# Neighbourhood heads of a two-layer encoder: borders transposed together, high and low parts stacked in one product, meta columns in one product

## The chip, the core and the metric

One program on one core of a Trainium2 chip. The metric is device time in microseconds of one execution, as the median of several; smaller is better. Beside it stands one profiled execution, whose span runs from the first to the last instruction of the program. The engines are PE (TensorE; PEld is its weight load), ACT (ScalarE), DVE (VectorE), POOL (GpSimd) and SP (SyncE, which issues nearly all DMAs).

## What is computed

Two layers over 512 grid tokens (8 rows by 64 columns) and 16 meta tokens, D = 1024. Each layer has a global attention branch (A), a neighbourhood attention branch (B), gates, and two output projections. The change lies in branch B, here cut to what matters:

```python
def neighbourhood_attention(q, k, v, rpb):          # 8 heads of 64
    # meta queries see the 16 meta keys only
    s_mm = einsum('bqhd,bmhd->bhqm', qm, km) * scale
    o_meta = einsum('bhqm,bmhd->bqhd', softmax(s_mm), vm)
    # a grid query sees a clamped window of 8 rows x 16 columns, with a bias, and the 16 meta keys
    s_win = einsum('bchd,bicjhd->bhcij', q_row, k_win) * scale + bias
    s_meta = einsum('bchd,bmhd->bhcm', q_row, km) * scale
    p = softmax(concatenate([s_win, s_meta], -1))
    o = einsum(p_win, v_win) + einsum(p_meta, vm)
```

All products are made from float32 values split into a high part (fp32r) and a low part (the remainder), so that `x*y` is high*high + high*low + low*high.

## The kernel before

**Main stream.** PE runs the projections (`product`, tiles `pp` and `y`, lines 391 to 393): for each chunk of 128 output columns, eight 128-row pieces times three products, into a bank of 256 and one of 272 tokens in layer 0, or one of 512 in layer 1. The weights come by DMA from SP (`raw`, L301), ACT makes the high part (`whi`, L306), POOL the low part (`wlo`, L307). At the end `pf` (L1306 to L1308) makes the last output product.

**Side work.** Two objects of class `Side` drop the attention work between these products. At each `tick` (twice per chunk) parts that are due are emitted. A neighbourhood head starts every fourth tick, and `NA_AT["stages"]` says at which tick after its start each stage is emitted: prepare 0, scores 2, transposes1 4, transposes2 5, transposes3 5, sums 7. Inside one engine the order is the scheduler's, moved at some places by the table `BEHIND`, which puts one named instruction behind another.

**A neighbourhood head** (`windowed_head`, 8 in each layer, 16 in all). The tokens are ordered column by column, so a window is a band. The scores of four blocks of 128 queries against 208, 272, 272 and 208 keys land in PSUM (`Sb`). DVE adds the bias and takes the maximum (L1062), ACT the exponential (L1064), in place in the 128x960 tile `bias`. Then PE transposes the probabilities by products with an identity (`transposed`, L196):

- `ta`: four 128x128 pieces of the inner keys; ACT and DVE split them into `tah` and `tal`.
- `tb`: two more inner pieces, and two of 80 columns from the borders (the first and the last 64 keys, each with a copy of the 16 meta keys); split into `tbh` and `tbl`.
- `tc`: one piece of 64 columns, in which the meta columns of the two inner query blocks lie; `split_meta` (L864 on ACT, L870 on DVE) puts it into the tile `na` with a mask `inner`.
- `tm` (layer 0 alone): the meta queries' own 16x16 probabilities, made from the two products `sm` (L627, L628), go to the tile `mm`.

The stage `sums` (L1124) then adds eleven products into one bank `avb` of 512 queries; the stationary operand is a slice of the values `VB2` (slices 0 to 2 inner, 3 and 4 borders, 5 the meta values). In layer 0 one product more, `avbm` (L1135), makes the meta queries' output. `window_edges` (L811) makes slices 3 to 5 of `VB2` once per pair of heads, from three transpositions `vtc` of 80 columns.

**Buffers around the change.** `na`, `mm`, `pm` are single buffers, zeroed once. The transposed pieces land in the PSUM pool `ps_t` with two banks; `S` and `Sb` share one double bank.

Of the kernel before, what the change touches and what calls it, by code (L numbers as in the profile page):

```python
# [38 lines left out]
NA_AT = ({"stages": (0, 2, 4, 5, 5, 7), "values": (3, 4), "divide": (3, 4, 7)},  # L39
         {"stages": (0, 2, 4, 5, 5, 7), "values": (3, 4), "divide": (3, 4, 7)})  # L40
# [18 lines left out]
BLK = ((0, 0, 208), (480, 64, 272), (208, 208, 272), (752, 336, 208))  # L59
# [3 lines left out]
BLK_META = 448  # L63
# [95 lines left out]
def trunk_kernel(ctx: ExitStack, tc: tile.TileContext, xT, w, gn, gf, bias, rope, out):  # L159
# [72 lines left out]
    for kind, (cols, n, dt) in {"ga": (256, 1, F32R), "na": (256, 1, F32R), "mm": (NMETA, 1, F32R), "pm": (32, 1, F32), "inv": (32, 1, F32)}.items():  # L232
# [9 lines left out]
    inner = cpool.tile([P, 1], F32, name="inner")  # L242
    nc.gpsimd.memset(inner, 1.0)
    nc.gpsimd.affine_select(inner, inner, pattern=[[0, 1]], compare_op=ALU.is_ge, fill=0.0, base=-NMETA, channel_multiplier=1)
    nc.gpsimd.affine_select(inner, inner, pattern=[[0, 1]], compare_op=ALU.is_ge, fill=0.0, base=3 * NMETA - 1, channel_multiplier=-1)
# [1142 lines left out]
```

## Time and profile before

| what | value |
|---|---|
| median of 3 runs | 819.23 us (818.29 to 820.59) |
| the profiled execution, its own time | 818.64 us |
| its span | 816.7 us |
| granted TensorE clock, mean | 0.999 |
| DVE, ACT, POOL busy | 505.2, 473.5, 418.0 us (62%, 58%, 51%) |
| PE products, weight loads | 5658 each |
| DMA moved | 134.99 MB, mean 165 GB/s |

How to read it: a product's record lasts longer than its turn, since the next one starts while it still drains. So the cost of a product on PE is the distance from its start to the start of the next, which the timeline view gives, and not the duration in its row. In timeline rows the columns are start and duration in us, engine, line, operation, tile written and tiles read, shape, and count. Rows with a bar are groups: busy time and mean of one, then idle time of the engine before them.

### The profile page before, as it was taken

What the parts mean: (1) busy time and instruction counts of PE and PEld (TensorE: products, weight loads), DVE (VectorE), ACT (ScalarE), POOL (GpSimd) and SP (SyncE); (2) the same over time, 40 slices, a digit from 0 to 9 for tenths busy, and PEclk for the clock granted to TensorE, in tenths of its full rate; (3) what the DMA queues carried; (4) which work ended last, traced back from release to release, by engine and by line L of the source; (5) the groups of instructions that cost most, each with busy time, mean ns of one, the idle gap of its engine ahead of it and who ended that gap; (6) DMA issues with size and microseconds to landing.
All of it is one profiled execution on the core that took longest, in us unless ns stands there. A gap on an engine that the chain in (4) does not pass through costs nothing.

```text
span 816.7 us, 16071 instructions
## 1 busy us (share of the span) xinstructions
PE 808.8 (99%) x5658; PEld 755.1 (92%) x5658; DVE 505.2 (62%) x1154; ACT 473.5 (58%) x1137; POOL 418.0 (51%) x362
## 2 busy tenths in 40 slices
PE   9999999999999999999999999999999999999997
PEld 9999999999999999999988989998988888888786
DVE  7566767796785662365547666676867655324733
ACT  8645777677865654443445557666758755544322
POOL 1654454454554544655754645554625555556651
PEclk9999999999999999999999999999999999999999
DMA  8347474667645563435555575766775555652602
GB/s 299 108 133 216 145 212 131 183 212 204 184 146 183 159 210 119 142 105 173 153 122 137 141 231 154 213 162 179 194 227 159 171 181 152 198 174 90 206 1 104
DMA packets 113248, 134.99 MB, mean 165 GB/s; under 512 B 31888, under 2 KB 66192, under 8 KB 113168
## 3 DMA queue, kind: packets, MB, share of 16 engines
q1 hardware_dynamic: 112448, 132.90, 54.9%
q8 instruction: 45, 0.74, 0.4%
q10 hardware_dynamic: 720, 1.06, 0.4%
q14 instruction: 35, 0.29, 0.1%
HBM read 98.50 MB, written 21.84 MB: 147 GB/s over the span
## 4 chain that ended last, share of the span: by engine, by line
PE 94%; DMA 2%; ACT 1%; DVE 1%; issue 1%; SPq 1%; POOLq 0%; POOL 0%; DVEq 0%; ACTq 0%
PE pp L393 20%; PE pp L391 20%; PE pp L392 20%; PE av L977 4%; PE y L393 4%; PE y L391 4%; PE y L392 4%; PE avb L1124 2%; PE S L627 2%; PE S L628 2%; PE pf L1306 2%; PE pf L1308 2%; PE pf L1307 2%; PE pp L516 2%; DMA raw<-in_w_dram 1%; PE Sb L628 1%
## 5 line engine op out<-in xcount | busy, mean ns | idle before, releaser
L307 POOL TENSOR_TENSOR wlo<-raw,whi 128x512 fp32r<-128x512 f32 x210 | 284.4, 1364 | 287.1 <-ACT whi L306 223.3
L391 PE MATMUL pp<-hh,whi 128*128 128x256 f32 (+2 forms) x1040 | 325.2, 313 | 0.0
L393 PE MATMUL pp<-hh,wlo 128*128 128x256 f32 (+2 forms) x1040 | 324.1, 312 | 0.0
L392 PE MATMUL pp<-hl,whi 128*128 128x256 f32 (+2 forms) x1040 | 323.4, 311 | 0.0
L393 PEld LDWEIGHTS pp<-hh,wlo 128*128 128x128 f32 x1040 | 195.7, 188 | 10.3
L392 PEld LDWEIGHTS pp<-hl,whi 128*128 128x128 f32 x1040 | 195.7, 188 | 9.3
L391 PEld LDWEIGHTS pp<-hh,whi 128*128 128x128 f32 x1040 | 195.9, 188 | 8.7
L306 ACT CAST whi<-raw 128x512 fp32r<-128x512 f32 x210 | 128.0, 619 | 106.3 <-PE pp L392 36.2
L970 POOL TENSOR_TENSOR ga<-pm,ga 32x128 fp32r<-32x128 f32 x64 | 39.4, 615 | 64.1 <-ACT ga L968 39.9
L939 DVE STREAM_TRANSPOSE P<-P 128x512 f32<-128x512 f32 x64 | 46.5, 727 | 29.8 <-ACT P L913 29.4
L1203 DVE TENSOR_TENSOR mg<-pp,rbc 128x256 f32<-128x256 f32 (+2 forms) x48 | 24.8, 516 | 54.0 <-PE pp L393 53.7
L909 DVE CUSTOM_DVE_ANT_0 P<-S,r 128x528 f32<-128x528 f32 x64 | 44.8, 701 | 15.5 <-PE S L628 14.7
L260 DVE TENSOR_TENSOR ptl<-P,pth 128x512 fp32r<-128x512 f32 x64 | 48.9, 780 | 4.7 <-ACT pth L259 4.2
L913 ACT ACTIVATE P<-P,st 128x528 f32<-128x528 f32 x64 | 47.2, 737 | 1.7
L1064 ACT ACTIVATE bias<-bias,stb 128x208 f32<-128x208 f32 (+1 forms) x64 | 31.0, 485 | 18.2 <-DVE stb L1062 18.2
L1204 ACT ACTIVATE mg<-mg 128x256 f32<-128x256 f32 (+2 forms) x48 | 23.6, 492 | 28.0 <-DVE mg L1203 27.9
L259 ACT CAST pth<-P 128x512 fp32r<-128x512 f32 x64 | 39.3, 614 | 0.9 <-DMA P<-turn 0.8
L392 PE MATMUL pp<-mx,whi 128*128 128x272 f32 (+1 forms) x128 | 36.4, 285 | 0.0
L391 PE MATMUL pp<-mx,whi 128*128 128x272 f32 (+1 forms) x128 | 36.4, 285 | 0.0
L393 PE MATMUL pp<-mx,wlo 128*128 128x272 f32 (+1 forms) x128 | 36.4, 285 | 0.0
L912 ACT ACTIVATE st<-st 128x1 f32<-128x1 f32 x64 | 12.9, 202 | 40.4 <-DVE st L909 40.1
L977 PE MATMUL av<-pth,VA 128*128 128x256 f32 x128 | 34.0, 289 | 0.0
(534 smaller groups left out, 1717.9 us busy)
## 6 DMA issues: line engine op xcount, KB each, us to landing
raw<-in_w_dram SPq DMA_DIRECT2D x210, 256.0 KB
turn<-P SPq DMA_DIRECT2D x32, 528.0 KB
P<-turn SPq DMA_DIRECT2D x128, 128.0 KB
bias<-in_bias_dram SPq DMA_DIRECT2D x16, 480.0 KB
KB<-KB SPq DMA_DIRECT2D x24, 272.0 KB
rawl<-in_w_dram SPq DMA_DIRECT2D x16, 256.0 KB
x<-in_xT_dram SPq DMA_DIRECT2D x8, 264.0 KB
xr<-in_xT_dram SPq DMA_DIRECT2D x8, 264.0 KB
```

Of the source, the lines that this page charges most:

```text
L259: split_at["hi"] = nc.scalar.copy(hi, src)
L260: split_at["any"] = nc.vector.tensor_sub(lo, src, hi.bitcast(F32))
L306: cast = nc.scalar.copy(hi, raw)
L307: sub = nc.gpsimd.tensor_sub(lo, raw, hi.bitcast(F32))
L391: nc.tensor.matmul(ps, wh, rh[:, a:b], start=i == 0, stop=False)
L392: nc.tensor.matmul(ps, wh, rl[:, a:b], start=False, stop=False)
L393: nc.tensor.matmul(ps, wl, rh[:, a:b], start=False, stop=i == n - 1)
L909: newest["max"] = nc.vector.tensor_tensor_reduce(p[:n], joined(S)[:n], scale[:n].to_broadcast([n, NTOK]), 1.0, -3e38, ALU.mult, ALU.max, s ...
L913: nc.scalar.activation(p[:n], p[:n], AF.Exp, bias=st[:n, 1:2], scale=1.0, accum_out=st[:n, 2:3] if total is None else total)
L939: nc.vector.transpose(c["both"][:n, a:b], c["both"][:n, a:b])
L970: nc.gpsimd.tensor_sub(tm[64 + 32 * t:96 + 32 * t, n * t:n * (t + 1)], m, tm[:32, :n].bitcast(F32))
L977: nc.tensor.matmul(c["av"], rows2(c["t"][i][0]), c["t"][i][1], start=i == 0, stop=i == 8)
```

## The change

Key order in a head is turned by half, so that the two borders lie next to each other in the tile `bias` (`BLK`, `ENDS` = 416) and 16-wide pads with the meta keys stay where the first and the inner blocks want them.

- **Borders.** One 128x128 transposition takes both borders (64 columns each) in place of two of 80 columns. Its result is split into the new tile `ne` of two halves: one for each border, with the high part on 64 partitions and the low part on the other 64. `window_edges` makes the slices 3 and 4 of `VB2` with the border's values twice, once on each 64 partitions. So the high and the low part of a border are summed in one product of 128x128, two per head in place of four of 80x128.
- **Metas.** POOL copies the four blocks' meta columns into the new tile `nm` (128x128, L1052 of the new kernel); one transposition of it, the fourth of `tb`, replaces `tc`, and `split_meta` writes four blocks of 16 rows into `na`, now 512 wide. One product of 128x512 in place of one of 128x256 adds all metas. `transposes3` is gone; the mask `inner` too.
- **Meta queries (layer 0).** Their probabilities are written into free columns of `nm`, so `tm` and the tile `pm` are gone; `mm` is filled from the same bank with a mask `upper`. The two products `sm` of 16x16 become one of 16x32 against the high and low keys side by side; ACT copies one half and DVE adds them.
- **Values.** `vtc` is two transpositions (128 and 64 columns) in place of three; ACT copies the halves across partitions.
- **Order.** The table `BEHIND` is written anew.

```diff
-BLK = ((0, 0, 208), (480, 64, 272), (208, 208, 272), (752, 336, 208))
+BLK = ((480, 0, 208), (0, 64, 272), (688, 208, 272), (272, 336, 208))
-BLK_META = 448
+ENDS, META_OF = 416, (1, 3, 0, 2)
...
-            for i, a in enumerate((0, EDGE, HD - NMETA)):
-                nc.tensor.transpose(ps[:EDGE, P * i:P * (i + 1)], v[:, a:a + EDGE], ident)
-            split(out[:EDGE, 3:, :, 0], out[:EDGE, 3:, :, 1], ps[:EDGE, :3 * P].rearrange("p (t h d) -> p t h d", t=3, h=2))
-            nc.scalar.copy(out[HD:, 5], out[:HD, 5].bitcast(F32))
+            nc.tensor.transpose(ps[:, :P], v[:, NKEY - P:], ident)
+            nc.tensor.transpose(ps[:HD, P:2 * P], v[:, :HD], ident)
+            src = ps[:, :2 * P].rearrange("p (t h d) -> p t h d", t=2, h=2)
+            split(out[:HD, 4:, :, 0], out[:HD, 4:, :, 1], src[:HD])
+            split(out[HD:, 3, :, 0], out[HD:, 3, :, 1], src[HD:, 0])
+            nc.scalar.copy(out[HD:, 4:], out[:HD, 4:].bitcast(F32))
+            nc.scalar.copy(out[:HD, 3], out[HD:, 3].bitcast(F32))
...
+                parts = [(slice(32 * i, 32 * i + NMETA), slice(P * b, P * b + P)) for i, b in enumerate(META_OF)]
+                for r, q in parts:
+                    nc.scalar.copy(to[:NMETA, q], tp[r])
+                for r, q in parts:
+                    nc.vector.tensor_sub(to[HD:HD + NMETA, q], tp[r], to[:NMETA, q].bitcast(F32))
...
+                c["nm"] = pad_tile("nm")
+                whole = c["bias"]
+                metas = bass.AP(whole.tensor, whole.offset, [whole.ap[0], (544, 2), (400, 2), (1, NMETA)])
+                with tc.high_priority():
+                    nc.gpsimd.tensor_copy(c["nm"].rearrange("p (i j t) -> p i j t", i=2, j=2)[:, :, :, :NMETA], metas)
...
-                    score(ps, c["q"], c["k"], slice(NREAL, NTOK), slice(HD, HD + NMETA))
+                    nc.tensor.matmul(ps, c["q"][:, NREAL:NTOK], c["k"][2][:, :, HD:HD + NMETA], start=True, stop=True)
...
+                    nc.scalar.copy(pm, ps[:, NMETA:])
+                    nc.vector.tensor_tensor_reduce(pm, ps[:, :NMETA], pm, -1.0, 3e38, ALU.add, ALU.min, sm[:, 0:1])
...
-                    transposed(ps[:, :P], c["pm"])
...
-                transposed(tp[:EDGE, 2 * P:3 * P], pb[0][:, :EDGE])
-                transposed(tp[:EDGE, 3 * P:4 * P], pb[3][:, P:P + EDGE])
...
-                split(bh[:, :256], bl[:, :256], tp[:, :256])
-                split(bh[:EDGE, 256:512], bl[:EDGE, 256:512], tp[:EDGE, 256:512])
...
-            def transposes3():
...
-                transposed(tp[:64, :P], c["bias"][:, BLK_META:BLK_META + 64])
...
-                split_meta([(tm[:, P:2 * P], tp[:, :P]), (tm[:, :P], tp[:, :P])], inner)
+                transposed(tp[:, 2 * P:3 * P], c["bias"][:, ENDS:ENDS + P])
+                transposed(tp[:, 3 * P:4 * P], c["nm"])
...
+                split(*c["b"], tp[:, :256])
...
+                    for (r, o), t in zip((rows(0), rows(1)), c["e"]):
+                        nc.scalar.copy(t[r], tp[r, 2 * P:3 * P])
+                    for (r, o), t in zip((rows(0), rows(1)), c["e"]):
+                        nc.vector.tensor_sub(t[o], tp[r, 2 * P:3 * P], t[r].bitcast(F32))
+                c["m"] = pad_tile("na")
+                split_meta(c["m"], tp[:, 3 * P:4 * P])
+                if full:
+                    ps, mh = tp[:32, 3 * P:3 * P + NMETA], pad_tile("mm")
+                    nc.vector.tensor_scalar_mul(mh[:32], ps, upper)
+                    nc.vector.scalar_tensor_tensor(mh[HD:HD + 32], ps, upper, mh[:32].bitcast(F32), op0=ALU.mult, op1=ALU.subtract)
...
-                seq = [(5, c["m"], 0, 128, 384)]
+                seq = [(5, c["m"], 0, 0, 512)]
                 for t in c["a"]:
                     seq += [(0, t, 0, 0, 256), (1, t, 256, 128, 384)]
                 for t in c["b"]:
-                    seq += [(2, t, 0, 256, 512), (3, t, 256, 0, 128), (4, t, 384, 384, 512)]
+                    seq += [(2, t, 0, 256, 512)]
+                seq += [(3, c["e"][1], 0, 0, 128), (4, c["e"][0], 0, 384, 512)]
```

What this makes of the engines' order is shown at three places. In these rows the first word is the line of that kernel, then operation, tile written, tiles read, shape and count; the first number in a tile's name is the head or chunk.

First PE, in layer 0, around the transpositions of head 1, before:

```order
L393 MATMUL pp_23_256_1751<-hh_7_231,wlo_23_1_1517 128x272
L196 MATMUL tb_1_1778<-ident,bias_1_1439 128x128 x2
L196 MATMUL tb_1_1778<-ident,bias_1_1439 80x128 x2
L196 MATMUL tc_1_1789<-ident,bias_1_1439 64x128
L391 MATMUL pp_7_0_1813<-hh_0_139,whi_7_0_1676 128x256
L392 MATMUL pp_7_0_1813<-hl_0_140,whi_7_0_1676 128x256
```

and PE at the same place now:

```order
L382 MATMUL pp_23_256_1749<-hh_7_232,wlo_23_1_1521 128x272
L187 MATMUL tb_1_1776<-ident,bias_1_1438 128x128 x3
L187 MATMUL tb_1_1776<-ident,nm_120 128x128
L380 MATMUL pp_7_0_1816<-hh_0_140,whi_7_0_1678 128x256
L381 MATMUL pp_7_0_1816<-hl_0_141,whi_7_0_1678 128x256
```

Five transpositions became four, and the last of them now reads the tile that POOL writes.

Second PE, in layer 1, at the sums of head 1, before:

```order
L393 MATMUL pp_23_0_7620<-hh_7_6341,wlo_23_1_7476 128x512
L1124 MATMUL avb_1_7666<-na_118,VB_0_7201 128x256
L1124 MATMUL avb_1_7666<-tah_1_7518,VB_0_7201 128x256 x2
L1124 MATMUL avb_1_7666<-tal_1_7519,VB_0_7201 128x256 x2
L1124 MATMUL avb_1_7666<-tbh_1_7579,VB_0_7201 128x256
L1124 MATMUL avb_1_7666<-tbh_1_7579,VB_0_7201 128x128 x2
L1124 MATMUL avb_1_7666<-tbl_1_7580,VB_0_7201 128x256
L1124 MATMUL avb_1_7666<-tbl_1_7580,VB_0_7201 128x128 x2
L391 MATMUL pp_7_0_7714<-hh_0_5821,whi_7_0_7610 128x512
```

and PE at these sums now:

```order
L382 MATMUL pp_23_0_7631<-hh_7_6346,wlo_23_1_7485 128x512
L1108 MATMUL avb_1_7677<-na_118,VB_0_7206 128x512
L1108 MATMUL avb_1_7677<-tah_1_7527,VB_0_7206 128x256 x2
L1108 MATMUL avb_1_7677<-tal_1_7528,VB_0_7206 128x256 x2
L1108 MATMUL avb_1_7677<-tb_1_7587,VB_0_7206 128x256 x2
L1108 MATMUL avb_1_7677<-ne_122,VB_0_7206 128x128 x2
L380 MATMUL pp_7_0_7723<-hh_0_5826,whi_7_0_7621 128x512
```

Eleven products became nine; the columns that stream through PE are 2304 in both.

Third DVE, in layer 1, behind the transpositions of the last head (7), before:

```order
L260 TENSOR_TENSOR tal_7_9264<-ta_7_9258,tah_7_9263 128x512
L260 TENSOR_TENSOR ptl_4_1_2_9200<-P_4_1_8947,pth_4_1_2_9199 128x8x2x32
L260 TENSOR_TENSOR tbl_7_9276<-tb_7_9270,tbh_7_9275 128x256
L939 STREAM_TRANSPOSE P_5_0_9145<-P_5_0_9145 128x512
L260 TENSOR_TENSOR tbl_7_9276<-tb_7_9270,tbh_7_9275 80x256
L870 SCALAR_TENSOR_TENSOR na_118<-tc_7_9281,inner,na_118 32x128 x2
```

and DVE behind the same transpositions now:

```order
L249 TENSOR_TENSOR tal_7_9288<-ta_7_9282,tah_7_9287 128x512
L249 TENSOR_TENSOR tb_7_9299<-tb_7_9294,tb_7_9299 128x256
L1088 TENSOR_TENSOR ne_122<-tb_7_9294,ne_122 64x128 x2
L852 TENSOR_TENSOR na_118<-tb_7_9294,na_118 16x128 x4
L249 TENSOR_TENSOR ptl_4_1_0_9167<-P_4_1_8966,pth_4_1_0_9166 128x8x2x32
L249 TENSOR_TENSOR ptl_4_1_2_9226<-P_4_1_8966,pth_4_1_2_9225 128x8x2x32
```

Four operations of the head became seven, all of them ahead of branch A's `ptl`, of which one stood ahead before. On PE 22 products of 128x512 and one of 128x256 stand between the last transposition and the sums of this head now, the shortest such distance in the new order.

More of the change, by code (lines that the diff above doesn't have):

```diff
@@ L38 @@
           {"scores": (0, 1), "turn": (1, 2), "back": 3, "split": (4, 5), "ends": 5, "divide": (2, 3, 6), "sums": (7, 7)})
-NA_AT = ({"stages": (0, 2, 4, 5, 5, 7), "values": (3, 4), "divide": (3, 4, 7)},
-         {"stages": (0, 2, 4, 5, 5, 7), "values": (3, 4), "divide": (3, 4, 7)})
+NA_AT = ({"stages": (0, 2, 4, 5, 7), "values": (3, 4), "divide": (3, 4, 7)},
+         {"stages": (0, 2, 4, 5, 7), "values": (3, 4), "divide": (3, 4, 7)})
 NORM_AT = ({"tokens": (0, 2, 4), "squares": (1, 1, 2, 3, 2), "heads": (2, 3, 5, 7, 6), "values": (1, 4)},
@@ L231, in trunk_kernel @@
     padded = {}
-    for kind, (cols, n, dt) in {"ga": (256, 1, F32R), "na": (256, 1, F32R), "mm": (NMETA, 1, F32R), "pm": (32, 1, F32), "inv": (32, 1, F32)}.items():
+    for kind, (cols, n, dt) in {"ga": (256, 1, F32R), "na": (NREAL, 1, F32R), "nm": (P, 1, F32), "ne": (2 * P, 1, F32R), "mm": (NMETA, 1, F32R), "inv": (32, 1, F32)}.items():
         padded[kind] = deque(cpool.tile([P, cols], dt, name=f"{kind}{i}") for i in range(n))
@@ L239, in pad_tile @@
         return padded[kind][0]
[L242 to L245, printed above, removed]
+    upper = cpool.tile([32, 1], F32, name="upper")
+    nc.gpsimd.memset(upper, 1.0)
+    nc.gpsimd.affine_select(upper, upper, pattern=[[0, 1]], compare_op=ALU.is_ge, fill=0.0, base=-NMETA, channel_multiplier=1)
     x1d = dpool.tile([NREAL, D], F32, name="x1d")
@@ L606, in stack_k @@
                 nc.sync.dma_start(t[to].bitcast(F32), one[r].bitcast(F32))
-            return [(t[:, 0], t[:, 1]) for t in (one, two_)]
+            return [(t[:, 0], t[:, 1], t) for t in (one, two_)]
         def stack_soon(tag, name, k, n, hh):
@@ L693, in pair_factors @@
         def pair_factors(t, c, n, name):
-            f = slot("G", f"pf{name}{l}") if n > 1 else tiny.tile([P, P], F32, tag="pf", bufs=1, name=f"pf{name}{l}")
+            f = slot("G", f"pf{name}{l}")
             f = f[:, :P * n].rearrange("p (n h d) -> p n h d", n=n, h=2)
@@ L839, in combine @@
             r, q = rows(hh)
-            t = slot(tag, f"cmb{nc.next_id()}")
+            t = slot(tag, f"cmb{nc.next_id()}") if n > NMETA else tiny.tile([P, NMETA], F32, tag="cmbm", name=f"cmbm{l}_{nc.next_id()}")
             nc.scalar.copy(t[r, :n], av[q, :n])
@@ L854, in rows2, with split_meta @@
             return v.rearrange("p s d -> p (s d)")
-        def split_meta(parts, keep=one):
+        def split_meta(to, tp):
             with tc.high_priority():
-                for g, (to, tp) in enumerate(parts):
-                    r = slice(32 * g, 32 * g + 32)
-                    if keep is one:
-                        nc.scalar.copy(to[r], tp[r])
-                    else:
-                        nc.scalar.mul(to[r], tp[r], keep[r])
-                for g, (to, tp) in enumerate(parts):
-                    r, low = slice(32 * g, 32 * g + 32), slice(64 + 32 * g, 96 + 32 * g)
-                    if keep is one:
-                        nc.vector.tensor_sub(to[low], tp[r], to[r].bitcast(F32))
-                    else:
-                        nc.vector.scalar_tensor_tensor(to[low], tp[r], keep[r], to[r].bitcast(F32), op0=ALU.mult, op1=ALU.subtract)
+                parts = [(slice(32 * i, 32 * i + NMETA), slice(P * b, P * b + P)) for i, b in enumerate(META_OF)]
[3 more added lines that the diff above has]
+                    nc.vector.tensor_sub(to[HD:HD + NMETA, q], tp[r], to[:NMETA, q].bitcast(F32))
         def divided_later(sums, gate, name):
@@ L1085, in transposes1 @@
                 split(c["a"][0][:, :512], c["a"][1][:, :512], tp)
-                if full:
-                    ps = bank(ps_t, f"tm{nm}", "tp")[:32]
-                    transposed(ps[:, :P], c["pm"])
-                    ps = ps[:, :NMETA]
-                    mh = pad_tile("mm")
-                    nc.vector.tensor_copy(mh[:32], ps)
-                    nc.vector.tensor_sub(mh[64:96], ps, mh[:32].bitcast(F32))
-                    c["mt"] = mh
             def transposes2():
@@ L1099, in transposes2 @@
                 transposed(tp[:, P:2 * P], pb[3][:, 0:P])
-                transposed(tp[:EDGE, 2 * P:3 * P], pb[0][:, :EDGE])
-                transposed(tp[:EDGE, 3 * P:4 * P], pb[3][:, P:P + EDGE])
-                c["b"] = bh, bl = slot("B", f"tbh{nm}", F32R), slot("B", f"tbl{nm}", F32R)
-                split(bh[:, :256], bl[:, :256], tp[:, :256])
-                split(bh[:EDGE, 256:512], bl[:EDGE, 256:512], tp[:EDGE, 256:512])
-            def transposes3():
-                tp = bank(ps_t, f"tc{nm}", "tp")
-                transposed(tp[:64, :P], c["bias"][:, BLK_META:BLK_META + 64])
-                c["m"] = tm = pad_tile("na")
-                split_meta([(tm[:, P:2 * P], tp[:, :P]), (tm[:, :P], tp[:, :P])], inner)
+                transposed(tp[:, 2 * P:3 * P], c["bias"][:, ENDS:ENDS + P])
+                transposed(tp[:, 3 * P:4 * P], c["nm"])
+                t, e = slot("B", f"tb{nm}", F32R), pad_tile("ne")
+                c["b"] = t[:, :256], t[:, 256:512]
+                split(*c["b"], tp[:, :256])
+                c["e"] = e[:, :P], e[:, P:]
+                with tc.high_priority():
+                    for (r, o), t in zip((rows(0), rows(1)), c["e"]):
[8 more added lines that the diff above has]
+                    nc.vector.scalar_tensor_tensor(mh[HD:HD + 32], ps, upper, mh[:32].bitcast(F32), op0=ALU.mult, op1=ALU.subtract)
+                    c["mt"] = mh
             def sums():
@@ L1119, in sums @@
                 for t in c["b"]:
[L1120 removed]
+                    seq += [(2, t, 0, 256, 512)]
+                seq += [(3, c["e"][1], 0, 0, 128), (4, c["e"][0], 0, 384, 512)]
                 for i, (u, t, c0, a, b) in enumerate(seq):
[L1123 to L1124 removed]
+                    nc.tensor.matmul(av[:, a:b], rows2(VB2[:, u, hh]), t[:, c0:c0 + b - a], start=i == 0,
                                      stop=i == len(seq) - 1, skip_group_check=True)
@@ L1136, in sums @@
                 ending.append(collect)
-            return prepare, scores, transposes1, transposes2, transposes3, sums
+            return prepare, scores, transposes1, transposes2, sums
         stacks = {"next": 0, "scored": 0}
@@ L1158, in window_values @@
                 kvq[j]["o"] = slot("B", f"ob{l}_{j}")
-                values(vb, kvq[j]["v2"], [(t, P * t + 2 * EDGE, P) for t in range(3)], f"b{l}_{j}")
+                values(vb, kvq[j]["v2"], [(t, P * t + 2 * NMETA, P) for t in range(3)], f"b{l}_{j}")
             else:
```

34 lines of the change are left out of this document (13 added, 21 removed), and 45 rows, old and new, of the table BEHIND.

## The prediction

> **What bounds the kernel now.** I read the page first: how long PE is busy, and whose work makes up the chain that ended last.
>
> ```profile
> span 816.7 us, 16071 instructions
> PE 808.8 (99%) x5658; PEld 755.1 (92%) x5658; DVE 505.2 (62%) x1154; ACT 473.5 (58%) x1137; POOL 418.0 (51%) x362
> PE 94%; DMA 2%; ACT 1%; DVE 1%; issue 1%; SPq 1%; POOLq 0%; POOL 0%; DVEq 0%; ACTq 0%
> ```
>
> PE is busy for 808.8 of 816.7 us and makes 94% of the chain; no other engine reaches two thirds. An average could hide a stage with another bound, so the next view is the table of stretches (length, PE busy, then PEld, DVE, ACT, POOL).
>
> ```profile
> 235.00:427.00 192.00, 192.00 (x1544) 190.22 (x1543) 101.62 (x195) 93.67 (x200) 102.33 (x84) 1.00 0.51 152
> 483.00:645.00 162.00, 160.91 (x1037) 144.97 (x1036) 114.91 (x285) 112.18 (x292) 81.36 (x70) 1.00 0.63 182
> 765.00:816.70 51.70, 45.87 (x222) 37.87 (x220) 21.41 (x39) 14.37 (x31) 21.79 (x17) 0.98 0.27 97
> ```
>
> In a stretch without neighbourhood heads PE has no idle time at all; in the stretch that holds the eight heads of layer 1 it idles for 162.00 - 160.91 = 1.09 us, and at the end of the program for 5.83 us, which the change does not touch. So time taken off PE is time taken off the program, as long as nobody else becomes late. A busy PE may still wait inside a record, so the price of each product has to come from distances between starts.
>
> **Transpositions: 32 fewer.** The timeline of PE, first where `tb` and `tc` of head 1 (layer 0) stand together, then where the `tc` of head 0 stands alone, and the groups with their counts:
>
> ```profile
> 110.48 0.29 PE L393 MATMUL pp<-hh,wlo 128*128 128x272 f32 x1
> 110.61 0.60 PE L196 MATMUL tb<-ident,bias 128*128 128x128 f32 x4
> 111.04 0.27 PE L196 MATMUL tc<-ident,bias 128*64 128x128 f32 x1
> 111.07 0.36 PE L391 MATMUL pp<-hh,whi 128*128 128x256 f32 x1
> 111.27 0.28 PE L392 MATMUL pp<-hl,whi 128*128 128x256 f32 x1
> 111.39 0.28 PE L393 MATMUL pp<-hh,wlo 128*128 128x256 f32 x1
> ...
> 95.67 0.27 PE L196 MATMUL tc<-ident,bias 128*64 128x128 f32 x1
> 95.69 0.36 PE L392 MATMUL pp<-hl,whi 128*128 128x256 f32 x1
> 95.90 0.27 PE L393 MATMUL pp<-hh,wlo 128*128 128x256 f32 x1
> ```
>
> ```profile
> L196 PE MATMUL tc<-ident,bias 128*64 128x128 f32 x16 | 4.4, 272 | 0.0
> L811 PE MATMUL vtc<-ident,vb 128*80 128x128 f32 x24 | 4.0, 274 | 0.0
> L196 PE MATMUL tm<-ident,pm 128*32 128x128 f32 x8 | 2.2, 273 | 0.0
> ```
>
> Four `tb` take 111.04 - 110.61 = 0.43 us, 0.108 each, though two are 80 wide and two 128: width does not matter. The last of a group seems to cost 0.03 us (111.04 to 111.07), but the `pp` behind it then takes 0.20 (to 111.27) where the next 256-wide one takes 0.12 (to 111.39): together 0.11 again. Alone it is the same: 0.02 for `tc`, then 0.21 in place of 0.12. So a transposition costs 0.109 us wherever it stands. All 16 `tc` and all 8 `tm` go, and 8 of 24 `vtc`; `tb` stays at four. 32 x 0.109 = **3.49 us** less.
>
> **Sums: 11 products become 9.** PE at the sums of head 1 in layer 1, the products behind them, and two rows from a plain stretch:
>
> ```profile
> 519.59 0.28 PE L1124 MATMUL avb<-na,VB 128*128 128x256 f32 x1
> 519.71 0.40 PE L1124 MATMUL avb<-tah,VB 128*128 128x256 f32 x2
> 519.95 0.40 PE L1124 MATMUL avb<-tal,VB 128*128 128x256 f32 x2
> 520.18 0.46 PE L1124 MATMUL avb<-tbh,VB 128*128 128x256 f32 x3
> 520.47 0.51 PE L1124 MATMUL avb<-tbl,VB 128*128 128x256 f32 x3
> 520.81 0.45 PE L391 MATMUL pp<-hh,whi 128*128 128x512 f32 x1
> 521.10 0.40 PE L392 MATMUL pp<-hl,whi 128*128 128x512 f32 x1
> ...
> 706.80 0.39 PE L391 MATMUL pp<-hh,whi 128*128 128x512 f32 x1
> ...
> 717.60 0.40 PE L393 MATMUL pp<-hh,wlo 128*128 128x512 f32 x1
> ```
>
> The first five, all 256 wide, take 520.18 - 519.59 = 0.59 us, 0.118 each. The other six end at 520.81, and the `pp` behind them takes 0.29. Of 512 columns the last two rows tell the plain price: they are the first and the last of 48 products of 512 in a row, 47 distances in 10.80 us, 0.230 each. So the six cost 0.63 + 0.06 = 0.69. Two of them are 256 wide (0.236), so the four of 128 columns cost some 0.45, **0.112 each**, nearly as much as 256 columns. Before: 7 x 0.118 + 4 x 0.112 = 1.274. Now: one of 512 (0.230), six of 256 (0.708), two of 128 (0.224): 1.162. The difference is 0.112 us a head, 16 x 0.112 = **1.79 us**.
>
> **Meta queries (layer 0).** Two `sm` become one of 32 columns:
>
> ```profile
> 134.62 0.17 PE L627 MATMUL sm<-KB,QB_1b 128*16 128x16 f32 x1
> 134.65 0.17 PE L628 MATMUL sm<-KB,QB_1b 128*16 128x16 f32 x1
> 134.67 0.37 PE L391 MATMUL pp<-hh,whi 128*128 128x272 f32 x1
> 134.88 0.29 PE L392 MATMUL pp<-hl,whi 128*128 128x272 f32 x1
> ```
>
> Each takes 0.03 us and the `pp` behind them 0.21, which is 0.08 more than the 0.13 between 110.48 and 110.61; that stays. One product less saves 0.026, eight times **0.2 us**. `avbm` keeps its form.
>
> The sum on PE is 3.49 + 1.79 + 0.2 = **5.48 us**: 3.3 in layer 0 (20 transpositions, 8 sums, 8 `sm`) and 2.2 in layer 1.
>
> [...]
>
> **What is added elsewhere.** One bank `tb` is now emptied by more, smaller operations: ACT 7 in place of 4 a head, DVE 7 in place of 4, and 2 for `mm` in layer 0 that stood elsewhere before. The nearest rows:
>
> ```profile
> L864 ACT ACTIVATE na<-tc,inner 32x128 fp32r<-32x128 f32 x32 | 11.5, 358 | 2.9 <-PE tc L196 2.6
> L870 DVE SCALAR_TENSOR_TENSOR na<-tc,inner,na 32x128 fp32r<-32x128 f32 x32 | 11.0, 344 | 1.8 <-ACT na L864 1.2
> L260 DVE TENSOR_TENSOR tal<-ta,tah 128x512 fp32r<-128x512 f32 x16 | 10.9, 678 | 2.0 <-ACT tah L259 1.8
> L260 DVE TENSOR_TENSOR tbl<-tb,tbh 80x256 fp32r<-80x256 f32 x16 | 6.7, 419 | 2.6 <-ACT tbh L259 2.5
> L644 POOL COPY qmt<-q 128x16 f32<-128x16 f32 x4 | 1.2, 320 | 1.4 <-DVE q L573 1.4
> ```
>
> A new 16x128 or 64x128 operation lies between 0 and 0.42 us; I take 0.35. Three more a head are 1.05 us on ACT and as much on DVE, some 17 us each over 16 heads, against 343 and 311 us of idle time there: covered, and nothing for the end of the program. POOL's copy of 4x16 columns is new; a 128x16 copy takes 0.32, so I take 0.5 (between 0.32 and four such, 1.3), 8 us over the program beside 398 us of idle time. It waits for the head's last exponential, and two new waits hang on it. On POOL the weight remainders `wlo` are queued behind it, which PE needs; they are made ahead of use, and POOL idles for half the span. On PE the fourth transposition of `tb` waits for it, with the whole main stream behind; but scores and `tb` lie three ticks apart, in layer 1 three times 12 products of 512, 36 x 0.230 = 8.3 us, and the copy adds 0.5 to what was there. The remaining edits on the values (more ACT and DVE pieces, on 64 partitions) are eight times about 1 us on idle engines and count nothing.
>
> The question is whether PE, coming to `avb`, finds `na` ready. Before, this wait was:
>
> ```profile
> PE avb L1124: 0.2, 1
> ```
>
> (who waited for `na`: 0.2 us, once, in 16 heads.) In the new order the shortest cover, in the last head of layer 1, is 22 products of 512 and one of 256: 22 x 0.230 + 0.118 = 5.2 us. The chain on DVE there is `tal`, `tb`, two `ne` and four `na`: 0.68 + 0.42 + 6 x 0.35 = 3.2 us, and ACT's beside it 7 x 0.36 = 2.5. Wholly one behind the other they would be 5.7, so the worst case there is 0.5 us late. What is late next is branch A's `ptl`, which the order now puts behind `na`: at most one of its 0.7 us.
>
> **Waits that may come or go.** The new order moves everything by a little. In layer 1 there are places where a transfer ends last:
>
> ```profile
> 560.13 6.10 DMA bias<-in_bias_dram
> ...
> 566.36 0.38 DVE L1062 CUSTOM_DVE_ANT_0 bias<-Sb,bias 128x208 f32<-128x208 f32 x1 [1.91 <-DMA bias<-in_bias_dram]
> ```
>
> This bias came 1.91 us late for DVE and cost PE most of the 1.09 us above. I take the waits as unchanged; the ends are 1.1 us less (all gone) and 4 us more (four heads with 1 us each).
>
> **The sum.** The profiled execution took 818.64 us itself: 816.7 of span and 1.9 around it. 818.64 - 5.48 = 813.2. The median of the runs is 0.6 above that execution, which would make it 813.8; I give the middle, **813.5**.
>
> **The rivals.**
> - *Layer 1 gives nothing*, since transfers set the pace there: the bias of 6.1 us and weights behind it. For it speaks the row of 1.91 us; against it that PE idles only 1.09 of 162 us. Then only layer 0's 3.3 us remain: 815.4. Chance 0.17, with other waits that eat 2 to 3 us.
> - *The change does not do what it says, as columns set the price.* A product would cost by its columns, 128 at half of 0.118: 32 x 0.059 = 1.9 us for the transpositions, nothing for the sums: 816.7. The 0.108 and 0.112 us speak against it. [...] Chance 0.05.
> - *No change that shows*, by several waits of 0.3 to 0.5 us a head that eat most of the gain: 816 to 821. Chance 0.07.
> - *Slower*: PE waits at `avb` for `na` in every head, because emptying `tb` is now longer than the cover between transpositions and sums. It decides from (5.48 + 2.46)/16 = 0.5 us a head; at 0.6 it would be 818.64 - 5.48 + 9.6 = 822.8. For it speak seven small operations in a row on two engines that are over half busy; against it the 5.2 us of the shortest cover and a wait of 0.2 us in all before. Chance 0.06.
>
> **How the numbers follow.** The forecast (811.5 to 815) has 0.62, the same with the waits gone (below 811.5) 0.03. Faster by over 0.3%, about what a measurement of this kernel tells from no change, takes these two and the first rival: 0.82; within it 0.12, slower 0.06. The range leaves out the last rivals' far ends: from 811.5 (813.2 less the 1.1 of waits is 812.1, and the fastest run lay 0.9 below the median) to 817.0, which holds the first two rivals and most of the 4 us of new waits.
>
> **What would show it.** In the profile after: 32 fewer transpositions and 40 fewer other products on PE, so 5586 in place of 5658; a `tb` group of four at 0.43 us with the `pp` behind it 0.08 longer; the nine products of `avb` at 1.16 us; PE busy near 803 us and the span near 811.3. If `avb` is late, the wait of PE for `na` shows more than 0.2 us; if POOL's copy hurts, weight products wait for `wlo`. Wrong would be: nine products that take 1.27 us, or idle time on PE over 2 us between 483 and 640 us.

## The result and the profile after

| kernel | median, us | range, us |
|---|---|---|
| before, beside it | 818.76 | 817.79 to 820.59 |
| after | 831.02 | 829.79 to 832.23 |

The ratio is 1.0147, with a 95% interval of 1.0122 to 1.0172: 12.3 us slower, where 5.5 us faster was forecast. From the page of the changed kernel:

```profile
span 828.1 us, 16078 instructions
PE 809.1 (98%) x5586; PEld 749.7 (91%) x5586; DVE 522.7 (63%) x1210; ACT 487.6 (59%) x1209; POOL 422.6 (51%) x378
```

PE has the 5586 products that were forecast, 72 fewer than before, and is still called busy for 809.1 us against 808.8. The span gives the account: 828.1 us where the prediction had 811.3, or some 17 us more. Of these, 11.1 are idle time of PE (828.1 - 809.1 = 19.0 us, against 816.7 - 808.8 = 7.9 before), and 5.8 are time inside PE's records (809.1, where 803.3 were to be left). The table of stretches (columns as above) says where:

```profile
235.00:427.00 192.00, 190.62 (x1532) 188.47 (x1533) 105.38 (x202) 92.77 (x201) 104.62 (x85) 1.00 0.53 153
483.00:645.00 162.00, 154.15 (x964) 136.19 (x963) 113.11 (x297) 113.33 (x308) 78.15 (x75) 1.00 0.60 176
```

The 1.38 us of idle time in the first row lie before 250 us, where the last head of layer 0 ends; behind it, without neighbourhood heads, nothing changed. In layer 1's heads PE now idles for 162.00 - 154.15 = 7.85 us, where it idled for 1.09. In layer 0's, from 80 to 235 us, it idles for 2.48 us, where it had no idle time at all. Part of each wait lies inside PE's records besides. The view of waits names, per pair of waiter and releaser, us in total, times, and the longest. Before:

```profile
PE S L627 <- DVE stb L1062: 0.8, 1, 0.8
PE avb L1124 <- DVE na L870: 0.2, 1, 0.2
PE av L977 <- DVE ptl L260: 0.2, 1, 0.2
```

and after:

```profile
PE avb L1108 <- DVE na L852: 4.2, 5, 1.6
PE S L616 <- DVE stb L1044: 4.0, 4, 1.9
PE av L959 <- ACT pth L248: 2.3, 2, 1.4
```

There are three kinds of wait: the sums wait for the metas (`na`), the global branch's scores wait for the bank `S` (which `stb`, the maxima of a neighbourhood head, set free), and the global branch's sums wait for `pth`. Only the first has to do with the changed data. One place of the second kind, in the timeline of the changed kernel, PE first:

```profile
552.00 0.28 PE L617 MATMUL Sb<-KB,QB_1b 128*128 128x208 f32 x1
...
554.01 0.29 PE L380 MATMUL pp<-hh,whi 128*128 128x272 f32 x1
556.15 0.39 PE L616 MATMUL S<-KA1h,Q 128*128 128x256 f32 x1 [1.85 <-DVE stb L1044]
```

ACT at that place:

```profile
550.89 0.52 ACT L1086 CAST ne<-tb 64x128 fp32r<-64x128 f32 x2
552.37 1.07 ACT L850 CAST na<-tb 16x128 fp32r<-16x128 f32 x4 [0.96 <-DVE ne L1088]
```

and DVE:

```profile
549.80 0.42 DVE L249 TENSOR_TENSOR tb<-tb,tb 128x256 fp32r<-128x256 f32 x1
551.02 0.71 DVE L921 STREAM_TRANSPOSE P<-P 128x512 f32<-128x512 f32 x1 [0.80 <-ACT P L895]
551.75 0.59 DVE L1088 TENSOR_TENSOR ne<-tb,ne 64x128 fp32r<-64x128 f32 x2
...
553.47 1.19 DVE L852 TENSOR_TENSOR na<-tb,na 16x128 fp32r<-16x128 f32 x4 [0.61 <-ACT na L850]
554.69 0.38 DVE L1044 CUSTOM_DVE_ANT_0 bias<-Sb,bias 128x208 f32<-128x208 f32 x1
```

Read it from the end. PE waits until 556.15 for the maxima, which start at 554.69. They stand in DVE's queue behind four subtractions `na`; these wait 0.61 us for ACT's four copies; those wait 0.96 us for DVE's `ne`; and `ne` stands behind a `STREAM_TRANSPOSE` of the global branch, which waited 0.80 us for ACT. The scores `Sb` that the maxima read were done long before: the last product of them starts at 552.00. But DVE does not take the maxima up ahead of `na`, which the program put in front. So a small operation at a queue's head, waiting for the other engine (0.61 us here), holds up what stands behind it.

That ACT's `na` waits for DVE's `ne` (0.96 us here, 5.6 us at seven places in all) is no matter of data: `ne` and `na` are different tiles. Both read the bank `tb`, and the program as it ran lets only one of the two engines at this bank at a time: in the whole trace none of ACT's 112 operations on it overlaps one of DVE's 128. So `tb` is emptied in six legs (turns of one engine at the bank): ACT `tb`, DVE `tb`, ACT `ne`, DVE `ne`, ACT `na`, DVE `na`. What an overlap would do, no run here shows.

### The profile page after: what moved, and what is told of

Its sections match the earlier page's. It is cut to its first block, busy times and chain, and to the rows that moved or that the text cites. A ratio compares the mean times of both kernels' runs of the same rounds, so it can differ in the third digit from the quotient of the medians.

```text
span 828.1 us, 16078 instructions
## 1 busy us (share of the span) xinstructions
PE 809.1 (98%) x5586; PEld 749.7 (91%) x5586; DVE 522.7 (63%) x1210; ACT 487.6 (59%) x1209; POOL 422.6 (51%) x378
## 4 chain that ended last, share of the span: by engine, by line
PE 65%; DVE 8%; ACT 7%; issue 3%; DMA 2%; SPq 1%; POOL 1%; POOLq 0%; DVEq 0%; ACTq 0%
PE pp L382 13%; PE pp L380 13%; PE pp L381 13%; PE y L382 4%; PE y L380 4%; PE y L381 4%; PE av L959 3%; DMA turn<-P 2%; PE pf L1290 2%; PE pf L1292 2%; PE pf L1291 2%; PE S L616 1%; PE S L617 1%; PE avb L1108 1%; DVE na L852 1%
## 5 line engine op out<-in xcount | busy, mean ns | idle before, releaser
L952 POOL TENSOR_TENSOR ga<-pm,ga 32x128 fp32r<-32x128 f32 x64 | 42.4, 663 | 93.4 <-ACT ga L950 51.5
L249 DVE TENSOR_TENSOR ptl<-P,pth 128x512 fp32r<-128x512 f32 x64 | 50.8, 800 | 8.0 <-ACT pth L248 6.2
L959 PE MATMUL av<-ptl,VA 128*128 128x256 f32 x128 | 33.4, 287 | 0.3 <-DVE ptl L249 0.3
```

The source lines that it names most:

```text
L249: split_at["any"] = nc.vector.tensor_sub(lo, src, hi.bitcast(F32))
L952: nc.gpsimd.tensor_sub(tm[64 + 32 * t:96 + 32 * t, n * t:n * (t + 1)], m, tm[:32, :n].bitcast(F32))
L959: nc.tensor.matmul(c["av"], rows2(c["t"][i][0]), c["t"][i][1], start=i == 0, stop=i == 8)
```

## Experiments

| run | median, us | against before (95%) |
|---|---|---|
| after | 831.02 | 1.0147 (1.0122 to 1.0172) |
| one_turn | 836.71 | 1.0214 (1.0193 to 1.0235) |
| two_turns | 830.25 | 1.0136 (1.0112 to 1.0160) |
| before_more_turns | 823.46 | 1.0053 (1.0035 to 1.0070) |
| before_one_turn | 819.40 | 1.0000 (0.9990 to 1.0009) |
| nm_on_dve | 832.43 | 1.0160 (1.0137 to 1.0183) |
| changed_no_table | 855.91 | 1.0446 (1.0431 to 1.0462) |
| before_no_table | 840.13 | 1.0243 (1.0221 to 1.0264) |
| few_ops | 819.65 | 1.0002 (0.9992 to 1.0011) |
| few_no_table | 838.95 | 1.0233 (1.0217 to 1.0249) |
| few_no_copy | 819.29 | 0.9996 (0.9987 to 1.0006) |
| no_low | 821.21 | 1.0020 (1.0011 to 1.0030) |
| few_on_dve | 825.50 | 1.0072 (1.0057 to 1.0087) |
| few_on_act | 828.10 | 1.0105 (1.0089 to 1.0120) |
| sums_later | 839.97 | 1.0250 (1.0235 to 1.0266) |
| na_last | 834.42 | 1.0181 (1.0166 to 1.0197) |
| before_idle_ops | 830.30 | 1.0125 (1.0109 to 1.0140) |
| before_idle_late | 845.00 | 1.0309 (1.0287 to 1.0331) |
| maxima_first | 826.93 | 1.0097 (1.0083 to 1.0110) |

Each ratio is against runs of the kernel before that were made beside that run. Their medians lie between 818.76 and 819.94 us, so a difference of some 1 us between two rows tells nothing.

**First theory: the hand-overs (H).** If alternating cost the time, fewer legs should give it back. one_turn keeps all 14 operations and has ACT do its seven first:

```diff
-                split(*c["b"], tp[:, :256])
...
+                    split_at["hi"] = nc.scalar.copy(c["b"][0], tp[:, :256])
+                    for (r, o), t in zip((rows(0), rows(1)), c["e"]):
+                        nc.scalar.copy(t[r], tp[r, 2 * P:3 * P])
+                    for r, q in parts:
+                        nc.scalar.copy(to[:NMETA, q], tp[r, 3 * P:4 * P])
+                    split_at["any"] = nc.vector.tensor_sub(c["b"][1], tp[:, :256], c["b"][0].bitcast(F32))
...
```

> The changed kernel with the same 14 operations that empty `tb`, only in another order: ACT makes `tb`, two `ne` and four `na` first, then DVE subtracts all seven. Theory H (hand-overs): what costs time is not the work of the small operations but that ACT and DVE empty one bank by turns (tb, ne, na: six legs), each leg standing behind what its queue holds. With two legs nearly all waits for `na`, `stb` and `pth` go: 815 to 819, 12 or more below the changed kernel; PE waits for `na` under 1 us in all. Theory O (the new table of the order): nothing is gained by this, 829 to 833. Theory W (the added work itself on ACT and DVE): the same operations remain, so at most 2 us less, 829 to 832. Theory P (POOL's copy `nm` blocks its queue): 829 to 833.

It came out at 836.71, outside all four ranges and 5.7 us slower than the changed kernel. The waits for `na` and `stb` shrank (4.2 to 2.2 and 4.0 to 2.5 us), but a new one took their place:

```profile
PE av L959 <- DVE ptl L249: 5.4, 7, 1.5
PE S L616 <- DVE stb L1044: 2.5, 4, 1.2
PE avb L1113 <- DVE na L1095: 2.2, 3, 0.9
```

Seven small operations in one block hold up the global branch's `ptl` behind them. So H falls as a theory of the whole. Four legs, with `na` alone apart:

> The changed kernel with four legs in place of six: ACT `tb` and `ne`, DVE `tb` and `ne`, ACT `na`, DVE `na`. Theory H: between, 820 to 826, since one of two hand-overs too many is gone. Theories O, W and P: as the changed kernel, 829 to 833.

830.25: no gain. The wait at the sums for `na` is nearly gone here (0.5 us), but PE now waits 2.8 us for `ptl`, in six places, and still 3.9 us for the bank `S`: taking away one wait did not shorten the program. Two more legs in the kernel before, where the first split of `tb` is made in two pieces of 128 columns:

> The kernel before, with nothing of the change, but the first half of `tb` (256 columns) emptied as two pieces of 128, so that ACT and DVE empty this bank in six legs in place of four; the operations are smaller, and two more a head. Theory H: slower than before by 4 to 12 us, 823 to 831, with new waits of PE for `tbl` or `na` at the sums. Theories O and P: as before, 817 to 821. Theory W: at most 2 us more, up to 821.

823.46, or 4.5 us slower, within H's range; but this run also adds one operation a head on either engine, and the next one, which takes two legs off the kernel before (both copies, then both subtractions), gains nothing:

> The kernel before with the two pairs that empty `tb` regrouped: both copies on ACT, then both subtractions on DVE; the same operations. From one_turn and before_more_turns: turns by themselves cost little, and long blocks make other work wait, so 818 to 823; a hand-over theory would have 814 to 817.

819.40. Turns alone are not the cause.

**POOL's copy (P)** was moved to DVE (`nc.gpsimd.tensor_copy` to `nc.vector.tensor_copy`):

> The changed kernel with the copy `nm` on DVE in place of POOL. Theory P: POOL's queue no longer stands behind the last exponential (29 us of waits there), so the waits of PE for `pth` go and the time falls by 3 to 6 us, to 825 to 828. Theory H: no gain; DVE now waits for ACT once more a head, 830 to 836. Theory O: 829 to 833.

832.43: P's gain does not show, and PE's wait for `pth` stays (2.6 us).

**The table (O).** Both kernels with `BEHIND = {}`:

> The changed kernel with the table BEHIND empty, so that the scheduler's own order stands. To be compared with the kernel before with an empty table. Theory O (the new pairs are the worse ones): with both tables empty the change gains what PE saves, so this run is 3 to 6 us below the other. Theory N (the number of small operations that ACT and DVE have to do ahead of other work costs, whatever the table): this run is 6 us or more above the other.

> The kernel before with the table BEHIND empty. What the old table is worth: an estimate is 5 to 15 us, so 824 to 834. Theory O: the changed kernel without its table is 3 to 6 us below this. Theory N: it is 6 us or more above this.

855.91 against 840.13. Without either table the change costs 15.8 us, with both 12.3. The old table is worth some 20 us to its kernel, more than estimated, and the new one some 25 to its own, so O falls: the new table is not the poorer one, and the loss is there without it. That a table searched further could win part of it back is not ruled out; three places are tried below.

**The number of small operations (N).** few_ops keeps PE's products, the six legs and the table, and makes three operations of seven on either engine (the kernel before has four, not three as the expectation says):

```diff
-                    for (r, o), t in zip((rows(0), rows(1)), c["e"]):
-                        nc.scalar.copy(t[r], tp[r, 2 * P:3 * P])
...
+                    nc.scalar.copy(e[:, :P], tp[:, 2 * P:3 * P])
+                    nc.vector.tensor_sub(e[:, P:], tp[:, 2 * P:3 * P], e[:, :P].bitcast(F32))
...
+                    nc.scalar.copy(to[:HD, :P], tp[:HD, 3 * P:4 * P])
+                    nc.vector.tensor_sub(to[HD:, :P], tp[:HD, 3 * P:4 * P], to[:HD, :P].bitcast(F32))
```

> The changed kernel with `ne` filled by one operation on ACT and one on DVE (128x128) in place of two each, and `na` by one each (64x128) in place of four each: three operations on either engine a head as before the change, still six legs. The borders' and metas' pieces do not land in their places, so this part of the output is left wrong; PE's products are the same. Theory N: most of the loss goes, 815 to 820. Theory O: as the changed kernel, 828 to 832. Theory H (hand-overs alone): 828 to 832.

819.65: 11.4 of the 12.3 us are gone. PE's waits for the bank `S` and for `pth` are gone from its view of waits, and the one for `na` is 1.3 us. The groups show what was taken away, first of the changed kernel (behind the bar: busy us, mean ns of one, then idle time before them):

```profile
L852 DVE TENSOR_TENSOR na<-tb,na 16x128 fp32r<-16x128 f32 x64 | 18.4, 288 | 10.9 <-ACT na L850 10.2
L850 ACT CAST na<-tb 16x128 fp32r<-16x128 f32 x64 | 16.5, 258 | 6.4 <-DVE ne L1088 5.6
L1088 DVE TENSOR_TENSOR ne<-tb,ne 64x128 fp32r<-64x128 f32 x32 | 9.2, 289 | 2.6 <-ACT ne L1086 2.0
L1086 ACT CAST ne<-tb 64x128 fp32r<-64x128 f32 x32 | 8.3, 259 | 5.0 <-DVE tb L249 4.8
```

and of few_ops:

```profile
L1090 DVE TENSOR_TENSOR na<-tb,na 64x128 fp32r<-64x128 f32 x16 | 4.5, 284 | 3.1 <-ACT na L1089 2.8
L1085 ACT CAST ne<-tb 128x128 fp32r<-128x128 f32 x16 | 4.2, 260 | 4.2 <-DVE tb L249 4.2
L1089 ACT CAST na<-tb 64x128 fp32r<-64x128 f32 x16 | 4.1, 257 | 5.1 <-DVE ne L1086 5.1
```

An operation on 16 partitions takes 258 ns on ACT, one on 128 partitions 260, so the work goes by the number of operations and not by their rows. The changed kernel's four groups are 27.6 us on DVE and 24.8 on ACT, and 25 us of standing idle ahead of them; in few_ops the same data take 8.9 and 8.3 us. The run takes away the number, the busy time and the standing idle together; which of these costs what, it does not separate.

> The kernel of few_ops (three operations on either engine a head; borders and metas misplaced) with the table BEHIND empty. Theory N holds whatever the table: 840 to 846, some 11 to 16 below the changed kernel without its table (855.9) and near the kernel before without its table (840.1). If few_ops was fast only because the new table happens to suit it: 850 or more.

838.95, 1 us below N's range, against 855.91 for the changed kernel without a table: the same finding without any table, 17 us.

Which engine's queue? Without DVE's six subtractions:

> The changed kernel without DVE's six subtractions a head for `ne` and `na` (the low parts of borders and metas are left out), ACT's six copies as they are. Theory N, if DVE's queue is the one that hurts: 813 to 818; if ACT's: 824 to 830. Theory O: 828 to 832. Theory H: four legs less, 815 to 820, so this run tells N on ACT from the others and few_ops tells N from H.

821.21, in none of these ranges, between N on DVE and N on ACT. It also has three legs in place of six, so the two halves of few_ops were run one at a time:

> The changed kernel with DVE's six subtractions for `ne` and `na` made as two larger ones (128x128 and 64x128), ACT's six copies as they are; the low parts don't land in their places. Theory N with DVE's queue as the one that hurts: 820 to 823. Theory N with both queues alike: 824 to 827, half of the 11.4 us that few_ops took off. Theory N with ACT's queue: 829 to 832.

> The other half: ACT's six copies for `ne` and `na` made as two larger ones, DVE's six subtractions as they are; the high parts don't land in their places. Theory N with DVE's queue as the one that hurts: 827 to 831. Both alike: 824 to 827. ACT's queue: 819 to 823.

825.50 and 828.10, that is 5.5 and 2.9 us off; together they are 8.4, where both at once take 11.4. The first lies in the range for both queues alike, the second in that for DVE's. Neither engine's pieces alone are the whole cause, and the gain of both at once is more than the sum. That each engine stands in the other's way is how the rows above read; no run measures it by itself.

**The rest of PE's saving.** few_ops equals the kernel before, though its PE has 5.5 us less to do. Was it POOL's copy?

> The kernel of few_ops without POOL's copy `nm` (the metas of the grid queries are left out of the sums). few_ops still lies 5 us above what PE's saving would give. If POOL's copy, which stands in its queue until the head's last exponential, takes the rest: 814 to 816. If the rest are other waits that a new order brings: 818 to 820.

819.29: no. Part of the rest shows as idle time of PE (817.6 - 806.9 = 10.7 us in few_ops, 7.9 before), in small waits (`av` for `ptl` 1.3 us, `avb` for `na` 1.3 us, others below that); another part lies inside PE's records, 806.9 us where 803.3 were to be left. What would remove them stays open.

**More room for the sums.** sums_later changes 7 to 8 in the stage table:

> The changed kernel, complete, with the stage `sums` one tick later (8 in place of 7), which gives the emptying of `tb` 12 more products of PE as cover. If the loss were the wait of PE at the sums for `na` alone (my rival of the prediction), 822 to 826 with no wait for `na` left. If the small operations make other work on the same queues late (`stb`, `ptl`, `pth`), those waits stay: 826 to 831.

839.97, 9 us slower than the changed kernel and outside both ranges, although the wait for `na` fell from 4.2 to 0.9 us. Every head's later stages now stand elsewhere, and the table was made for the old places; this run tells only that later sums don't help as they stand. na_last moves the products of `ne` and `na` to the end of the nine (two products start the bank then, and the output is no longer that of the changed kernel, so the kernel is not complete as the expectation has it):

> The changed kernel, complete, with the same nine products of the sums in another order: `tah` and `tb` first, `ne` and `na` last, so that `na` may come some 0.9 us later without a wait. If the wait at the sums for `na` is one part of the loss: 4 of its 5 places shrink by up to 0.9 us, 827 to 829. If it is nothing: 830 to 832.

834.42, above both ranges. The wait for `na` fell from 4.2 to 2.3 us, but the sums now wait for `ne` (1.2 us) and others, 4.7 us in all, and the waits for the bank `S` rose from 4.0 to 5.5 us.

**Small operations that nobody waits for.** In the kernel before, four 16x128 operations a head on either engine behind the first split of `tb`, into scratch:

```diff
                 split(bh[:, :256], bl[:, :256], tp[:, :256])
...
+                    for i in range(4):
+                        nc.scalar.copy(sa, bl[:NMETA, :P].bitcast(F32))
+                    for i in range(4):
+                        nc.vector.tensor_sub(sd, bl[:NMETA, :P].bitcast(F32), bh[:NMETA, :P].bitcast(F32))
```

> The kernel before, complete, with four small operations (16x128) more a head on ACT and four on DVE behind the first split of `tb`, into scratch that nobody reads. If it is enough that the two queues hold more small operations there (place and time on the engine): 825 to 831. If what costs is that the sums wait for the last of a longer chain: the scratch is on no chain, so 818 to 821.

830.30, 10.7 us slower, with nothing of the change in it. PE's waits of that kernel:

```profile
PE S L627 <- DVE stb L1062: 3.7, 4, 1.3
PE av L977 <- DVE ptl L260: 1.7, 4, 0.5
PE avb L1130 <- DVE na L870: 1.4, 2, 0.9
```

The wait for the maxima is there as in the changed kernel (3.7 and 4.0 us, four times each). So the loss needs neither POOL's copy nor the new table, only more operations in the two queues. The scratch is not wholly without effect on the sums: their wait for `na` rose from 0.2 to 1.4 us, and some of ACT's copies stand ahead of its second split of `tb`. The size is no clean copy either: these subtractions read SBUF and take 471 ns in the mean, those of the change 288.

> The kernel before, complete, with the same number of small operations as before_idle_ops (four of 16x128 a head on DVE, four on ACT), but behind the sums, at ordinary priority, where no maximum and no sum stands right behind them; they write scratch. If place decides: 819 to 823. If the number of operations on the two queues decides wherever they stand: 826 to 831.

845.00, outside both ranges. This edit had a fault as an experiment: here ACT's scratch copies read DVE's scratch, and ACT stands at its queue's head for 23.9 us:

```profile
L1133 ACT COPY xa<-xd 16x128 f32<-16x128 f32 x64 | 18.9, 296 | 25.0 <-DVE xd L1131 23.9
```

It tells that small operations behind the sums are not free either. Whether the place or ACT's waiting made it worse than before_idle_ops, it does not tell, nor does it separate place from number.

**The order at one place.** In the changed kernel, complete, twelve pairs put DVE's `na` of heads 0, 2 and 6 of layer 1 behind the next head's maxima (the first four shown):

```diff
+        ("na0", 32, "bias1_1", 3), ("na0", 33, "bias1_1", 3), ("na0", 34, "bias1_1", 3), ("na0", 35, "bias1_1", 3),
```

> The changed kernel, complete, with twelve more pairs in the table: in heads 0, 2 and 6 of layer 1 the four subtractions `na` on DVE stand behind the next head's maxima (`stb`) and no longer ahead of them. If the loss there is the queue's order (maxima that stand behind small operations which still wait for ACT, while the bank `S` stays taken and PE waits): three places with 0.75, 2.1 and 1.6 us lie there, so 826 to 828.5, and the sums of these heads, which had 3 us in hand, don't wait. If the waits are only shifted to the next place: 830 to 832.

826.93, 4.1 us less, of 4.45 us that lay at the three places. DVE of that kernel, at the place shown above:

```profile
551.03 0.59 DVE L1088 TENSOR_TENSOR ne<-tb,ne 64x128 fp32r<-64x128 f32 x2
...
552.06 0.36 DVE L1044 CUSTOM_DVE_ANT_0 bias<-Sb,bias 128x208 f32<-128x208 f32 x1
...
553.48 1.19 DVE L852 TENSOR_TENSOR na<-tb,na 16x128 fp32r<-16x128 f32 x4
```

and its PE, and its view of waits:

```profile
553.31 0.29 PE L380 MATMUL pp<-hh,whi 128*128 128x272 f32 x1
553.50 0.39 PE L616 MATMUL S<-KA1h,Q 128*128 128x256 f32 x1
```

```profile
PE avb L1108 <- DVE na L852: 4.2, 5, 1.6
PE av L959 <- ACT pth L248: 2.6, 3, 1.4
PE S L616 <- DVE stb L1044: 0.9, 2, 0.5
```

This kernel is 0.72 us further on at this place (`ne` starts at 551.03, and at 551.75 behind the old order). The maxima start at 552.06, before `na`. ACT's copies `na` run from 551.65 to 552.71, so DVE's `na`, which start at 553.48 behind the maxima, were held back by 0.77 us. Nobody waits for them: the sums of this head start at 555.09. PE's wait for the bank fell from 4.0 to 0.9 us, while its waits for `na` (4.2 us) and `pth` (2.6) stayed. It is the fastest complete version of the change, and still slower than the kernel before; no run here beats that one.

## Why the prediction was wrong, step by step

**PE's sum of 5.48 us: right.** The nine products of the sums in layer 1, where nothing waits:

```profile
508.53 0.40 PE L1108 MATMUL avb<-na,VB 128*128 128x512 f32 x1
508.77 0.39 PE L1108 MATMUL avb<-tah,VB 128*128 128x256 f32 x2
...
509.47 0.33 PE L1108 MATMUL avb<-ne,VB 128*128 128x128 f32 x2
509.64 0.33 PE L380 MATMUL pp<-hh,whi 128*128 128x256 f32 x1
509.81 0.28 PE L381 MATMUL pp<-hl,whi 128*128 128x256 f32 x1
```

They take 509.64 - 508.53 = 1.11 us, and the `pp` behind them 0.17 where a plain one takes 0.12: 1.16, as forecast. Four transpositions in layer 1 take from 547.40 to 547.76, and the product behind them 0.21 in place of 0.11: 0.115 each, near the 0.109 taken. The count of 5586 held, and the columns did not set the price, so that rival falls; what sets the price of a narrow product, no run takes apart. "PE busy near 803" was wrong, since the part of a wait that lies inside a product's record counts as busy: the record at 554.01 us above lasts 0.29 us, where the one before it gave way after 0.13 (553.88 to 554.01), so 0.16 us of that wait are called busy.

**"Covered, and nothing for the end of the program": the step that failed.** The size of the added work was right: DVE is busy for 17.5 us more and ACT for 14.1, where some 17 were forecast. Each operation was priced too high, if anything (0.35 us taken; 0.26 on ACT, 0.29 on DVE measured). The error was to set this work against 343 and 311 us of idle time. That idle time is an average, and most of it lies where an engine stands at its queue's head for somebody else: in the kernel before, waits for other engines and for transfers make 316 of ACT's 343 us and 297 of DVE's 311. few_ops is the test of this step: the same products and legs with three operations on either engine (four before the change, seven after), and 11.4 us are gone, where the prediction put nothing.

**The chain to `na`: "at most 5.7, the worst case 0.5 us late".** I counted the durations of six legs and nothing between them. One of the late places in the changed kernel, PE, then ACT, then DVE:

```profile
613.94 0.40 PE L380 MATMUL pp<-hh,whi 128*128 128x512 f32 x1
615.91 0.47 PE L1108 MATMUL avb<-na,VB 128*128 128x512 f32 x1 [1.57 <-DVE na L852]
```

```profile
608.75 0.36 ACT L248 CAST tb<-tb 128x256 fp32r<-128x256 f32 x1
...
611.11 0.52 ACT L1086 CAST ne<-tb 64x128 fp32r<-64x128 f32 x2
613.48 1.07 ACT L850 CAST na<-tb 16x128 fp32r<-16x128 f32 x4 [1.85 <-DVE ne L1088]
```

```profile
610.13 0.41 DVE L249 TENSOR_TENSOR tb<-tb,tb 128x256 fp32r<-128x256 f32 x1
...
611.24 1.58 DVE L823 SCALAR_TENSOR_TENSOR zb<-zb_3t,zb 128x512 f32<-128x512 f32 x1 [0.24 <-ACT zb_3t L818]
612.85 0.59 DVE L1088 TENSOR_TENSOR ne<-tb,ne 64x128 fp32r<-64x128 f32 x2
...
614.58 1.19 DVE L852 TENSOR_TENSOR na<-tb,na 16x128 fp32r<-16x128 f32 x4 [1.13 <-ACT na L850]
```

From ACT's first copy (608.75) to the end of DVE's last `na` (614.58 + 1.19) it is 7.0 us, for 4.1 us of work. The rest is other work that got in at the hand-overs, a gate of 1.58 us (`zb`) among it. The order that I quoted from DVE's queue showed what stands in front; what I left out is that every leg waits for the other engine, whose queue has its own things in front.

**"What is late next is branch A's `ptl`": incomplete.** Late next were the maxima, and through the bank `S` PE itself; maxima_first shows this part, 4.1 us. What holds up `pth`, the third wait, no run takes apart. I had looked for who waits for `na`, not for who stands behind it in DVE's queue.

**"I take the waits as unchanged", +4 us at most:** wrong by the sum of the three rows of PE's waits after, 10.5 us against 1.2 before, and by what of them lies inside records.

**POOL: right.** The copy took 0.29 us where 0.5 was taken, and without it few_ops stays the same.

**The rival "Slower"** named the right bank and the wrong width. PE waits at `avb` in 5 of 16 heads, for 4.2 us: 4.0 of the 9.3 us that the three rows grew by, and far from "every head". The rest comes from work that has nothing to do with the sums. "Idle time on PE over 2 us between 483 and 640 us", named as what would prove the forecast wrong, is what came.

## What to carry to other kernels

An added operation was not free here because its engine idles for 40% (DVE 38%, ACT 42% before the change): price it by what stands behind it in that queue. Small operations took their time by their number here, not by their rows (on ACT 258 ns on 16 partitions, 260 on 128), so a change that trades products on PE for pieces on ACT and DVE has to count those pieces: eight fewer a head were worth 11.4 us, twice what PE had saved. Where a stall comes from the order in a queue, moving the few operations that are not yet needed behind the one that frees a resource can get its price back: here 4.1 us of 4.45.

## What was not expected of the hardware

The 64 scratch subtractions of before_idle_ops, all of one shape, took 0.28 us in the median, 0.47 in the mean and up to 1.37. Two of them on DVE:

```profile
569.54 0.28 DVE L1109 TENSOR_TENSOR xd<-tbl,tbh 16x128 fp32r<-16x128 f32 x1
...
571.00 1.37 DVE L1109 TENSOR_TENSOR xd<-tbl,tbh 16x128 fp32r<-16x128 f32 x1
```

and POOL at that time:

```profile
569.95 2.27 POOL L894 TENSOR_TENSOR zb<-zb,sumsb 128x512 f32<-128x512 f32 x1 [1.73 <-DMA sumsb<-thereb]
```

The long one begins inside POOL's operation and ends 0.15 us after it (572.37 and 572.22). The gate of 1.58 us above is a like case: of the eight gates of that shape on DVE (L823, 128x512) in the changed kernel, the four that overlap no operation of POOL took 0.69 us each; of the four that overlap one, three took 0.97, 1.41 and 1.58, the last beside POOL's `wlo` and `zb`, and one 0.68. Of its 64 `ptl` of 128x512, 13 overlap none and took 0.64 to 0.69 us, and 51 overlap one and took 0.65 to 1.75. All these read both inputs from SBUF. The changed kernel's 64 subtractions `na` read one input from PSUM: the 32 that overlap an operation of POOL took 281 to 297 ns, the other 32 took 281 to 296, and the mean is 288. So operations on DVE with both inputs in SBUF could take longer beside POOL in these traces, and `na` did not; why, no run here shows.
